# Weight rounding in a two-layer encoder trunk: from a ScalarE copy to a converting transfer from DRAM, from the eighth slab on

## The chip, the core and the metric

The kernel runs on one core of a Trainium2 chip. The metric is the device time of one execution in microseconds (us). Engines are named as in the profile: PE is TensorE (matmuls), DVE is VectorE, ACT is ScalarE, POOL is GpSimd, SP is SyncE, whose queue issues most transfers.

## What is computed

The reference is an encoder trunk of two layers over x, 512 tokens of 1024 features in float32. Layer 0 has a combined mixer (a state-space scan with 16 heads and an mLSTM with 8 heads, each forward and backward), layer 1 a gated linear attention. Each layer ends in a convolutional feed-forward block (FFN):

```
def _conv_ffn(h, w_up, conv_w, conv_b, w_down):
    u = _dwconv(h @ w_up, conv_w, conv_b)
    gate, val = jnp.split(u, 2, axis=-1)
    return (jax.nn.gelu(gate, approximate=True) * val) @ w_down

def reference(...):
    for i in range(DEPTH):
        h = _rmsnorm(x, norm_g[i, 0])
        h = _ssd_mlstm_mixer(h, ...) if i % 2 == 0 else _gla_mixer(h, ...)
        x = x + _rmsnorm(h, norm_g[i, 1])
        f = _conv_ffn(_rmsnorm(x, norm_g[i, 2]), ffn_w_up[i], ffn_conv_w[i], ffn_conv_b[i], ffn_w_down[i])
        x = x + _rmsnorm(f, norm_g[i, 3])
    return x
```

All of the work is float32, and almost all of it is products with weights.

## The kernel before

All weights are laid out in order of use as 234 slabs of 128 x 1024 float32 (512 KB). A slab holds eight 128 x 128 tiles, mostly one output row tile of a product. PE multiplies in the type fp32r (a rounded float32). To keep float32 accuracy each operand is split in two parts: `hi`, the value rounded to fp32r, and `lo`, what is left. `mm3` makes three matmuls of the parts: hi by hi, hi by lo, lo by hi.

`w_load(i)` asks for slab i on SP's queue into `raw` (W_RAW = 3 buffers). `w_prep` makes `hi` on ACT (`S.copy`) and `lo` on DVE (raw minus hi), each in W_SPLIT = 5 buffers. `w_take` keeps W_AHEAD = 4 slabs made ahead of the one in use. So slab i's `hi` and `lo` can be written when the last matmul of slab i-5 is done, and they are read when four more slabs have gone through PE.

Products run as `Job`s (one slab, one PSUM bank) or as `nat_job`s (two slabs, four blocks of tokens). When a job ends, DVE takes its PSUM bank out (`conv` does so first of all) and then works on the result in SBUF. The eight banks have three names: two `pj`, three `ps`, three `pm`. FFN jobs go round all eight in turn (`PA`), the projections of the layer 0 mixer use the two `pj` alone.

The mixer of layer 0 first projects (slabs 0 to 11), then makes rows of gates in a long chain of DVE operations (`gate_rows`), writes them to DRAM (`rowd`, `rowd2`, `decd`), and loads them back spread over the partitions (SP's `s<-rowd` transfers of 256 KB). POOL multiplies some of these (`s160`, `s186`, `s191`, `s163`), and adds sums of squares (`accx`) at the ends of stages. Slabs 12 to 14 are three of the convolved projections (`s96`, `s100`, `s104` are their banks taken out), and 15 to 18 the z projection. Slabs 0 to 68 belong to mixer 0, 69 to 134 to FFN 0, 135 to 167 to mixer 1, and 168 to 233 to FFN 1. Between stages the first four FFN jobs run on half the tokens together, so their four slabs are needed at once.

The program is written in Tile: a scheduler sets the order of each engine's instructions from the program and its own estimates, and puts in the semaphore waits. Each engine then runs its list strictly in that order. All calls go through a recording helper, so nearly every instruction carries its line, L105. Instructions are told apart by their tiles.

Of the kernel before, what the change touches and what calls it, by code (L numbers as in the profile page):

```python
# [16 lines left out]
P = 128  # L17
T = 512
# [11 lines left out]

# columns of the constant block
_C = {}
# [8 lines left out]
class _Balance:  # L41
    """Work issued so far to TensorE and VectorE, in ns, to weave two streams evenly."""

# [3 lines left out]
    def weave(self, streams, done):  # L47
        """streams: (generator, engine whose work it is paced by, total ns of that work, head start in ns).
        The stream least far along goes on, if what it needs is done."""
        st = [{"g": g, "e": e, "n": float(n), "t": -lead / float(n), "need": None} for g, e, n, lead in streams]  # L50
        while st:
            ok = [x for x in st if x["need"] is None or x["need"] in done]
            assert ok, [x["need"] for x in st]
            x = min(ok, key=lambda x: x["t"])
            t0 = getattr(self, x["e"])
            try:
                x["need"] = next(x["g"])
            except StopIteration:
                st.remove(x)
            x["t"] += (getattr(self, x["e"]) - t0) / x["n"]  # L60


class _Life:
    """First and last use of every work tile, in program order, and from that a slot for each."""

# [15 lines left out]
    def plan(self, slots):  # L81
        """The slot that has been free for longest."""
        until, res = [-1] * slots, []
        for a, z in zip(self.first, self.last):
            i = min(range(slots), key=lambda j: until[j])
            assert until[i] < a or until[i] < 0, "too few slots"
            until[i] = z + 1
            res.append(i)
        return res


class _Eng:
    """An engine that notes which tiles its instructions touch and how long they take."""

# [36 lines left out]
def kernel(ctx: ExitStack, tc: tile.TileContext, xin, wst, cst, dsk, gw2, out, life=None, plan=None):  # L131
# [47 lines left out]

# [1 line left out]
    cc = cp.tile([P, NCONST], F32, name="cc")  # L181
# [30 lines left out]

# [1 line left out]
    wstate = {"raw": {}, "next": 0, "ready": [], "unit": 0}  # L214
    NSLAB = wst.shape[0]

    def w_load(i):
        raw = wp.tile([P, 1024], F32, tag="raw", name=f"raw{i}", bufs=W_RAW)
        SY.dma_start(raw, wst[i])
        wstate["raw"][i] = raw  # L220

    def w_prep():
        i = wstate["next"]
        if i >= NSLAB:
            return
        wstate["next"] += 1
        if i not in wstate["raw"]:
            w_load(i)
        raw = wstate["raw"].pop(i)
        hi = wp.tile([P, 1024], F32R, tag="hi", name=f"hi{i}", bufs=W_SPLIT)  # L230
        lo = wp.tile([P, 1024], F32R, tag="lo", name=f"lo{i}", bufs=W_SPLIT)
        S.copy(hi, raw)
        V.tensor_tensor(lo, raw, hi, ALU.subtract)
        wstate["ready"].append((hi, lo))

    def w_take(n, width=P):
        """The next n tiles of `width` columns of the stream, as (hi, lo) pairs."""
        res = []
        for _ in range(n):
            c0 = wstate["unit"]  # L240
            i, o = divmod(c0, 1024)
            while len(wstate["ready"]) < i + 1 + W_AHEAD and wstate["next"] < NSLAB:
                w_prep()
            hi, lo = wstate["ready"][i]
            res.append((hi[:, o:o + width], lo[:, o:o + width]))
            wstate["unit"] += width
        return res

    def mm3(o, a, b, first, last):
        """o += a^T b with operands in two exact parts."""  # L250
        (ah, al), (bh, bl) = a, b
# [7 lines left out]
    class Job:  # L259
        """One 128-row tile of W^T h."""  # L260

# [37 lines left out]
    def run_group(jobs, r, mid=None, serial=False):  # L299
        """Several jobs together, one k tile after the other (or one job after the other)."""  # L300
        if not serial:
# [42 lines left out]
    def nat_job(h, post, hi=False):  # L344
        """256 columns of h^T W with tokens on the partitions."""
        w = w_take(KD, 256)
# [12 lines left out]

# [1 line left out]
    def col_sum(o, i, acc):  # L361
        """o[tok, 2i + t]: the sum of acc[:, tok] over the partitions, for two tiles of tokens."""
        for t in range(2):
            PE.matmul(o[:, 2 * i + t:2 * i + t + 1], acc[:, t * P:(t + 1) * P], ones[:, 0:1], start=True, stop=True)

    def rstd(v, rs):
        """rs = 1 / sqrt(v / D + eps) for columns v."""
        S.activation(rs, v, AF.Sqrt, bias=eps1, scale=1.0 / D)
        V.reciprocal(rs, rs)

    def spread(o, rs):
        """o[p, tok] = rs[tok] on every partition."""
        for t in range(2):
            PE.matmul(o[:, t * P:(t + 1) * P], rs[:, t:t + 1].broadcast_to((P, P)), ident, start=True, stop=True)

    def split(xk, g, h, n, r):
        """The two exact parts of x * g (the norm's per-token factor is applied to the products)."""
        if h[n] is None:
# [5 lines left out]
    class Scale:  # L384
        """1 / rms of x for every token: as columns [tok, tile] and as a row on all partitions."""

# [28 lines left out]
    class Post:  # L415
        """x += f * g * rstd, fed with f one row tile and one token half at a time."""

# [26 lines left out]
        def finish(self, r, nxt=None):  # L444
            """nxt: (layer, which, h) of the norm that follows."""
            o = ps()
# [10 lines left out]

# [1 line left out]
    def conv(o, sc, wc, b, taps):  # L459
        """Depthwise convolution along the tokens of a PSUM tile, scaled by token, into SBUF."""  # L460
        half = taps // 2
# [54 lines left out]

# [1 line left out]
    def mixer0(h, x_again, sc, chain_of):  # L518
        done = set()
        # small block: dt and gates  # L520
        smallj = {}
# [22 lines left out]

# [1 line left out]
        rows = {}  # L546
# [11 lines left out]
        def gate_rows():  # L558
# [6 lines left out]
            V.reciprocal(d, d)  # L565
            V.tensor_tensor(u, u, d, ALU.mult)           # z = e / (2 + e)
            z2 = st()
            S.activation(z2, u, AF.Square)
            V.tensor_scalar(d, z2, 2.0 / 15, 2.0 / 13, ALU.mult, ALU.add)
            for j in range(5, -1, -1):  # L570
                V.tensor_tensor(d, d, z2, ALU.mult)
                V.tensor_scalar(d, d, 2.0 / (2 * j + 1), None, ALU.add)
            V.tensor_tensor(u, u, d, ALU.mult)           # log1p(exp(-|g|))
            lo64, hi64 = slice(0, 64), slice(64, 128)
# [32 lines left out]
            yield  # L607
            # SSD rows
            cs = st()
# [13 lines left out]
            yield  # L623
            # mLSTM rows
            ig = st()
# [30 lines left out]
            S.activation(q4[hi64], fc[hi64], AF.Exp)  # L656
            # rows to DRAM for broadcasts over the partitions
            G.dma_start(rowd[lo64], cs[lo64])
# [7 lines left out]
            G.dma_start(dskb, dsk.broadcast_to((P, 16)))  # L666
            # columns: [tok, chunk, (quantity of the pair, direction), head]
            for w, tiles in ((16, (q1, q2)), (8, (q3, q4))):
# [10 lines left out]

# [1 line left out]
        zt = [[None] * 2 for _ in range(NCH)]  # L681
# [12 lines left out]

# [1 line left out]
        def b8(ap):  # L696
# [150 lines left out]

# [1 line left out]
        kT, qT = [None] * 8, [None] * 8  # L849
# [143 lines left out]

# [1 line left out]
        part = [None] * KD  # L995
# [45 lines left out]

# [1 line left out]
    def mixer1(h, x_again, sc, chain_of):  # L1043
# [34 lines left out]
        def after(ins, first):  # L1078
            """Issue order only: groups activations by their function table."""
            tc.add_manual_dep(ins.ins, first.ins.name, mybir.DependencyInfo(  # L1080
# [58 lines left out]
        def head(hd, ps):  # L1139
# [7 lines left out]
            for dd in range(2):  # L1147
                bcv = bcs[dd][hd]
                b3 = bcv.rearrange("p (c l) -> p c l", l=64)
                ei = 63 if dd == 0 else 0  # L1150
                # first / second 64 tokens of a block in the order of the scan
                fi, se = (0, 1) if dd == 0 else (1, 0)
# [10 lines left out]
                after(S.activation(ke, ke, AF.Exp, scale=1.0 / 16.0), pin["ln"])  # L1163
                # kc: keys of the first half to its end, of the second half as they are
                kc, q2 = st(), st()
# [18 lines left out]
                yield  # L1184
                # whole-block operands of the states
                d2 = dec.rearrange("p (c u) -> p c u", u=2)
# [84 lines left out]

# [1 line left out]
    def load_x(src):  # L1273
# [8 lines left out]
    def load_first(r):  # L1282
        """Half the tokens of x, two row tiles to a tile."""
        x = [st() for _ in range(KD // 2)]
# [69 lines left out]
W_SPLIT = 5  # L1354
W_AHEAD = 4
BANKS = {"pj": 2, "ps": 3, "pm": 3}
PA = ("pj", "pm", "ps", "ps", "pm", "pj", "pm", "ps")
# [6 lines left out]
def _layout(a):  # L1364
    """Host-side layout: transposed activations, weights in the order of use, packed vectors."""
    f = lambda n: np.asarray(a[n])
# [84 lines left out]
def build(new, arrays):  # L1451
    """The program: traced once to learn how long each tile is in use, then with a slot for each."""
    plan = None
# [25 lines left out]
```

## Time and profile before

| | |
|---|---|
| time, median of 3 runs | 1556.7 us (1555.45 to 1556.77) |
| span of the profiled execution | 1554.8 us |
| PE busy | 1508.2 us, 97% |
| DVE busy | 1032.1 us, 66% |
| ACT busy | 730.6 us, 47% |
| POOL busy | 142.8 us, 9% |
| bytes read from HBM | 146.42 MB |

The span goes from the first to the last instruction. The profile gives no other time for that execution, and the runs stand 0.7 to 2.0 us above its span. An engine's busy time is an average over stages: what an edit is worth has to be read in its stage.

### The profile page before, as it was taken

The numbers are of one execution on the slowest core, as the hardware profiler recorded it, in microseconds if no ns is written. First come the engines' busy times: TensorE is split into PE (matmuls) and PEld (weight loads), VectorE is DVE, ScalarE is ACT, GpSimd is POOL, SyncE is SP. The second block draws the span as 40 slices with busy tenths as digits, with TensorE's granted clock in tenths as the row PEclk, the third lists the DMA queues.
The fourth block names the chain that finished last, engine by engine and source line by source line (L and its number), as shares of the span: only waits on it lengthen the run. The fifth ranks groups of instructions, "written<-read, shape, count | busy, mean of one in ns | idle before, by whom it ended". The sixth has DMA issues, their size and how long they took to land.

```text
span 1554.8 us, 22022 instructions
## 1 busy us (share of the span) xinstructions
PE 1508.2 (97%) x8616; PEld 1300.3 (84%) x8616; DVE 1032.1 (66%) x1703; ACT 730.6 (47%) x1332; POOL 142.8 (9%) x165
## 2 busy tenths in 40 slices
PE   7989999999999999999999999999999999999997
PEld 6879887888987988888888997898899888888887
DVE  6986789967754888623676378737537974267744
ACT  6445545744642664423444356436545543244432
POOL 5020321212100110000000030000003000000000
PEclk9999999999999999999999999999999999999999
DMA  5243243334322322222222132211131322222211
GB/s 186 96 156 96 82 129 102 102 114 140 131 91 79 112 86 104 95 95 95 95 95 99 69 123 103 74 56 55 65 125 69 109 95 95 95 95 95 95 69 54
DMA packets 67303, 152.46 MB, mean 98 GB/s; under 512 B 6256, under 2 KB 32896, under 8 KB 67200
## 3 DMA queue, kind: packets, MB, share of 16 engines
q1 hardware_dynamic: 61984, 145.77, 27.7%
q10 hardware_dynamic: 4752, 4.23, 0.9%
q8 instruction: 67, 1.10, 0.3%
q0 software_dynamic: 464, 1.06, 0.2%
q14 instruction: 36, 0.29, 0.1%
HBM read 146.42 MB, written 4.59 MB: 97 GB/s over the span
## 4 chain that ended last, share of the span: by engine, by line
PE 80%; DVE 11%; ACT 4%; DMA 3%; issue 2%; POOL 0%; SPq 0%; DVEq 0%; ACTq 0%; POOLq 0%
PE pj L105 31%; PE ps L105 25%; PE pm L105 24%; DVE s L105 8%; DMA s<-rowd 2%; ACT s L105 2%; DVE lo L105 2%; DVE t L105 1%; ACT hi L105 1%; ACT L105 0%; DVE pacc L105 0%; DMA raw<-in_w 0%; POOL s L105 0%; ACT msq L105 0%; DVE rd L105 0%
## 5 line engine op out<-in xcount | busy, mean ns | idle before, releaser
L105 DVE TENSOR_TENSOR lo<-raw,hi 128x1024 fp32r<-128x1024 f32 x234 | 291.4, 1249 | 220.5 <-ACT hi L105 220.3
L105 PE MATMUL pj<-s,hi 128*128 128x512 f32 (+1 forms) x1384 | 405.4, 376 | 5.2 <-ACT s L105 5.2
L105 ACT CAST hi<-raw 128x1024 fp32r<-128x1024 f32 x234 | 244.3, 1048 | 241.7 <-PE pj L105 107.7
L105 PE MATMUL pm<-s,hi 128*128 128x512 f32 (+1 forms) x1140 | 309.9, 357 | 8.4 <-ACT s L105 6.8
L105 PE MATMUL ps<-s,hi 128*128 128x512 f32 (+1 forms) x1140 | 307.3, 356 | 0.7 <-DVE t L105 0.7
L105 PEld LDWEIGHTS pj<-s,hi 128*128 128x128 f32 x1384 | 248.7, 189 | 54.6 <-ACT s L105 5.6
L105 PE MATMUL pj<-s,lo 128*128 128x512 f32 (+1 forms) x692 | 257.3, 372 | 0.0
L105 PE MATMUL pj<-hi,s 128*128 128x256 f32 x1280 | 241.6, 286 | 6.6 <-DVE s L105 3.0
L105 PEld LDWEIGHTS pm<-s,hi 128*128 128x128 f32 x1140 | 202.7, 190 | 41.6 <-ACT s L105 6.8
L105 PEld LDWEIGHTS ps<-s,hi 128*128 128x128 f32 x1140 | 202.2, 190 | 33.2 <-issue 1.1
L105 PEld LDWEIGHTS pj<-hi,s 128*128 128x128 f32 x1280 | 200.4, 189 | 9.1 <-DVE s L105 3.6
L105 PE MATMUL ps<-s,lo 128*128 128x512 f32 (+1 forms) x570 | 203.0, 356 | 1.2 <-DVE lo L105 1.2
L105 PE MATMUL pm<-s,lo 128*128 128x512 f32 (+1 forms) x570 | 203.1, 356 | 0.0
L105 PE MATMUL pj<-lo,s 128*128 128x256 f32 x640 | 180.7, 282 | 0.0
L105 DVE SCALAR_TENSOR_TENSOR s<-s,cc,s 128x511 f32<-128x511 f32 (+1 forms) x240 | 168.0, 712 | 3.2 <-ACT s L105 0.8
L105 ACT ACTIVATE s<-s 128x512 f32<-128x512 f32 (+1 forms) x145 | 90.3, 629 | 154.8 <-DVE s L105 137.0
L105 DVE TENSOR_TENSOR s<-s,s 128x512 f32<-128x512 f32 (+3 forms) x214 | 136.3, 651 | 34.0 <-ACT s L105 31.9
L105 PEld LDWEIGHTS pj<-s,lo 128*128 128x128 f32 x692 | 130.6, 189 | 23.8 <-issue 1.0
L105 ACT ACTIVATE s<-s,cc 128x512 f32<-128x512 f32 (+2 forms) x188 | 121.8, 664 | 38.2 <-DVE s L105 37.3
L105 PEld LDWEIGHTS ps<-s,lo 128*128 128x128 f32 x570 | 108.2, 190 | 17.6 <-DVE lo L105 1.6
L105 PEld LDWEIGHTS pj<-lo,s 128*128 128x128 f32 x640 | 121.5, 190 | 1.5 <-issue 1.0
L105 PEld LDWEIGHTS pm<-s,lo 128*128 128x128 f32 x570 | 108.3, 190 | 15.8
(155 smaller groups left out, 1342.5 us busy)
## 6 DMA issues: line engine op xcount, KB each, us to landing
raw<-in_w SPq DMA_DIRECT2D x234, 512.0 KB, 3.2
s<-rowd SPq DMA_DIRECT2D x64, 256.0 KB, 3.8
s<-in_x SPq DMA_DIRECT2D x8, 256.0 KB, 6.0
s<-in_x ACTq DMA_DIRECT2D x16, 128.0 KB, 2.7
xsave<-s SPq DMA_DIRECT2D x16, 128.0 KB, 2.3
s<-xsave ACTq DMA_DIRECT2D x16, 128.0 KB, 2.4
out_x<-s SPq DMA_DIRECT2D x16, 128.0 KB, 1.8
rowd<-s POOLq DMA_DIRECT2D x3, 128.0 KB, 2.3
```

The costliest lines, as they stand in the source:

```text
L105: return f(*a, **k)
```

## The change

From slab 8 on (`W_ACT = 8`) `hi` is no longer written by ACT. `w_load` issues a second transfer of the same slab from DRAM, on POOL's queue, whose target has the type fp32r, so the transfer rounds. `lo` is made on DVE as before, now from two transferred tiles. Slabs 0 to 7 stay with ACT. The other lines of the diff remove comments.

```
     def w_load(i):
         raw = wp.tile([P, 1024], F32, tag="raw", name=f"raw{i}", bufs=W_RAW)
         SY.dma_start(raw, wst[i])
-        wstate["raw"][i] = raw
+        hi = None
+        if i >= W_ACT:
+            hi = wp.tile([P, 1024], F32R, tag="hi", name=f"hi{i}", bufs=W_SPLIT)
+            G.dma_start(hi, wst[i])
+        wstate["raw"][i] = raw, hi
 ...
-        raw = wstate["raw"].pop(i)
-        hi = wp.tile([P, 1024], F32R, tag="hi", name=f"hi{i}", bufs=W_SPLIT)
+        raw, hi = wstate["raw"].pop(i)
+        if hi is None:
+            hi = wp.tile([P, 1024], F32R, tag="hi", name=f"hi{i}", bufs=W_SPLIT)
+            S.copy(hi, raw)
         lo = wp.tile([P, 1024], F32R, tag="lo", name=f"lo{i}", bufs=W_SPLIT)
-        S.copy(hi, raw)
         V.tensor_tensor(lo, raw, hi, ALU.subtract)
 ...
+W_ACT = 8
```

226 casts leave ACT, 226 issues come to POOL, and the scheduler sets DVE's, PE's and SP's instructions anew around them. Three places show it.

POOL's list after the gate rows, before the change (`s150` is the spread copy of `decd`, and the four products multiply rows loaded from `rowd2`):

```order
L105 DMA decd_1407<-dec129_1256 128x4
L105 DMA rowd2_513<-s87_920 64x512
L105 DMA s150_1409<-decd_1407 128x512
L105 TENSOR_TENSOR s160_1450<-s160_1450,s67_614 128x512
L105 TENSOR_TENSOR s186_1548<-s186_1548,s69_647 128x512
L105 TENSOR_TENSOR s191_1594<-s191_1594,s69_647 128x512
L105 TENSOR_TENSOR s163_1463<-s163_1463,s67_614 128x512
```

The same place of POOL's list with the change:

```order
L105 DMA rowd2_513<-s87_920 64x512
L105 DMA hi15_783<-in_w 128x1024
L105 DMA hi16_939<-in_w 128x1024
L105 DMA s150_1409<-decd_1407 128x512
L105 TENSOR_TENSOR s160_1450<-s160_1450,s67_614 128x512
L105 TENSOR_TENSOR s186_1548<-s186_1548,s69_647 128x512
L105 TENSOR_TENSOR s191_1594<-s191_1594,s69_647 128x512
L105 DMA hi17_981<-in_w 128x1024
L105 DMA hi18_1023<-in_w 128x1024
L105 TENSOR_TENSOR s163_1463<-s163_1463,s67_614 128x512
```

The transfers of slabs 15 and 16 now stand behind the issue of `rowd2`, and those of 17 and 18 behind three products that each wait for a loaded row.

DVE's list at the same time of the program, before the change (`pj95`, `pj99` and `pj103` are the banks of slabs 12, 13 and 14):

```order
L105 TENSOR_TENSOR lo16_940<-raw16_937,hi16_939 128x1024
L105 TENSOR_TENSOR s96_968<-pj95_943,srow9_127 128x512
L105 TENSOR_TENSOR lo17_982<-raw17_979,hi17_981 128x1024
L105 SCALAR_TENSOR_TENSOR s97_970<-s96_968,cwh43_238,s97_970 128x510
L105 SCALAR_TENSOR_TENSOR s97_970<-s96_968,cwh43_238,s97_970 128x511 x2
L105 SCALAR_TENSOR_TENSOR s97_970<-s96_968,cwh43_238,s97_970 128x510
L105 TENSOR_TENSOR s100_1010<-pj99_985,srow9_127 128x512
```

DVE's list there with the change:

```order
L105 TENSOR_TENSOR lo16_941<-raw16_937,hi16_939 128x1024
L105 TENSOR_TENSOR s96_968<-pj95_943,srow9_127 128x512
L105 SCALAR_TENSOR_TENSOR s97_970<-s96_968,cwh43_238,s97_970 128x510
L105 SCALAR_TENSOR_TENSOR s97_970<-s96_968,cwh43_238,s97_970 128x511 x2
L105 TENSOR_TENSOR lo17_983<-raw17_979,hi17_981 128x1024
L105 SCALAR_TENSOR_TENSOR s97_970<-s96_968,cwh43_238,s97_970 128x510
L105 TENSOR_TENSOR s100_1010<-pj99_985,srow9_127 128x512
```

`lo17` has moved behind three operations of the convolution, and it still stands ahead of `s100`, which takes the next bank out.

DVE's list in FFN 0, before the change (two jobs: one bank taken out into `s930`, the next into `s933`):

```order
L105 TENSOR_TENSOR s930_7169<-ps929_7144,srow42_237 128x512
L105 TENSOR_TENSOR lo111_7179<-raw111_7176,hi111_7178 128x1024
L105 SCALAR_TENSOR_TENSOR s931_7171<-s930_7169,cc_72,s931_7171 128x511 x2
L105 TENSOR_TENSOR s933_7207<-pj932_7182,srow42_237 128x512
L105 TENSOR_TENSOR lo112_7221<-raw112_7218,hi112_7220 128x1024
L105 SCALAR_TENSOR_TENSOR s934_7209<-s933_7207,cc_72,s934_7209 128x511 x2
```

The same two jobs with the change:

```order
L105 TENSOR_TENSOR s930_7169<-ps929_7144,srow42_237 128x512
L105 SCALAR_TENSOR_TENSOR s931_7171<-s930_7169,cc_72,s931_7171 128x511 x2
L105 TENSOR_TENSOR lo111_7180<-raw111_7176,hi111_7178 128x1024
L105 TENSOR_TENSOR s933_7207<-pj932_7182,srow42_237 128x512
L105 SCALAR_TENSOR_TENSOR s934_7209<-s933_7207,cc_72,s934_7209 128x511 x2
```

In each FFN job `lo` has gone from directly behind the taking out of the bank to behind the convolution's two operations.

## Rows read from the trace of the kernel before

**Rows 1.** The page: busy us of each engine, share of the span, instructions.

```profile
PE 1508.2 (97%) x8616; PEld 1300.3 (84%) x8616; DVE 1032.1 (66%) x1703; ACT 730.6 (47%) x1332; POOL 142.8 (9%) x165
```

**Rows 2.** Windows: busy us of PE, PEld, DVE, ACT, POOL; clock, DMA share, GB/s.

```profile
76.00:112.00 36.00, 31.36 (x181) 27.42 (x179) 31.00 (x42) 15.55 (x27) 8.66 (x9) 0.95 0.49 157
112.00:545.00 433.00, 419.54 (x2697) 368.91 (x2697) 318.81 (x622) 228.97 (x537) 77.02 (x65) 1.00 0.34 107
545.00:895.00 350.00, 349.58 (x1651) 289.26 (x1650) 212.63 (x279) 146.32 (x199) 6.59 (x10) 1.00 0.26 93
895.00:1200.00 305.00, 298.01 (x2059) 270.66 (x2059) 194.79 (x378) 157.90 (x318) 30.40 (x38) 0.99 0.24 82
```

**Rows 3.** DVE's timeline in FFN 0: start, us, operation, idle before it.

```profile
752.62 0.69 DVE L105 TENSOR_TENSOR s<-pj,srow 128x512 f32<-128x512 f32 x1 [2.02 <-PE pj L105]
753.47 1.23 DVE L105 TENSOR_TENSOR lo<-raw,hi 128x1024 fp32r<-128x1024 f32 x1 [0.16 <-ACT hi L105]
```

**Rows 4.** The page's groups: count, busy, mean ns, idle before by releaser.

```profile
L105 DVE TENSOR_TENSOR lo<-raw,hi 128x1024 fp32r<-128x1024 f32 x234 | 291.4, 1249 | 220.5 <-ACT hi L105 220.3
...
L105 ACT CAST hi<-raw 128x1024 fp32r<-128x1024 f32 x234 | 244.3, 1048 | 241.7 <-PE pj L105 107.7
```

**Rows 5.** The chain that ended last, by line, whole span.

```profile
PE pj L105 31%; PE ps L105 25%; PE pm L105 24%; DVE s L105 8%; DMA s<-rowd 2%; ACT s L105 2%; DVE lo L105 2%; DVE t L105 1%; ACT hi L105 1%; ACT L105 0%; DVE pacc L105 0%; DMA raw<-in_w 0%; POOL s L105 0%; ACT msq L105 0%; DVE rd L105 0%
```

**Rows 6.** That chain in order of time: start, us, what.

```profile
62.83 1.06 ACT hi L105
63.92 1.23 DVE lo L105
...
92.29 0.93 ACT hi L105
...
415.26 0.94 ACT hi L105
...
741.47 5.56 PE ps L105 x24
```

**Rows 7.** DMA issues (KB each, median us to landing), and POOL's time for one.

```profile
raw<-in_w SPq DMA_DIRECT2D x234, 512.0 KB, 3.2
s<-rowd SPq DMA_DIRECT2D x64, 256.0 KB, 3.8
...
s<-decd POOLq DMA_DIRECT2D x1, 256.0 KB, 5.7
...
s<-in_g POOLq DMA_DIRECT2D x1, 128.0 KB, 2.4
...
L105 POOL DMA_DIRECT2D rowd<-s x3 | 1.7, 562 | 44.9 <-DVE s L105 33.0 <-DVE ue L105 11.2 <-ACT s L105 0.7
```

**Rows 8.** POOL's timeline after the gate rows.

```profile
90.22 0.54 POOL L105 DMA_DIRECT2D rowd<-s  x1 [0.73 <-ACT s L105]
...
99.54 1.29 POOL L105 TENSOR_TENSOR s<-s,s 128x512 f32<-128x512 f32 x1 [7.79 <-DMA s<-rowd]
103.10 3.01 POOL L105 TENSOR_TENSOR s<-s,s 128x512 f32<-128x512 f32 x2 [2.27 <-DMA s<-rowd]
```

**Rows 9.** DVE's timeline there: slabs 16 and 18, banks of slabs 12 and 14.

```profile
93.26 1.22 DVE L105 TENSOR_TENSOR lo<-raw,hi 128x1024 fp32r<-128x1024 f32 x1 [0.63 <-ACT hi L105]
96.75 0.69 DVE L105 TENSOR_TENSOR s<-pj,srow 128x512 f32<-128x512 f32 x1 [2.27 <-PE pj L105]
...
98.78 4.17 DVE L105 SCALAR_TENSOR_TENSOR s<-s,cwh,s 128x510 f32<-128x510 f32 x4
...
104.87 2.32 DVE L105 TENSOR_TENSOR lo<-raw,hi 128x1024 fp32r<-128x1024 f32 x1
...
111.04 0.68 DVE L105 TENSOR_TENSOR s<-pj,srow 128x512 f32<-128x512 f32 x1
```

**Rows 10.** Start of FFN 0: `lo` of slab 72 on DVE, and PE's idle time.

```profile
528.25 1.22 DVE L105 TENSOR_TENSOR lo<-raw,hi 128x1024 fp32r<-128x1024 f32 x1
...
534.46 0.48 PE L105 MATMUL ps<-s,hi 128*128 128x256 f32 x2 [0.33 <-DVE t L105]
```

## The prediction

> **What bounds the kernel now.** I read the page's busy times first. PE is busy for 1508.2 of 1554.8 us [rows 1], so only 46.6 us of the span can be won by any edit that leaves the matmuls alone, and ACT, from which this change takes work, is at 47%. The windows by stage say where those 46.6 us lie. FFN 0 (545 to 895) has 0.4 us of idle PE in 350. The gate stage (76 to 112) has 4.6, the rest of mixer 0 (112 to 545) 13.5 and mixer 1 with its ends 7.0 [rows 2]. That makes 25.1 us of idle PE between 76 and 1200; what is left lies mostly at the start, which the change doesn't touch, and at the end. Then I read the chain of waits. The casts `ACT hi` have 1% of it and the loads `s<-rowd` 2% [rows 5]. The cast is 1.05 us long and there are 234 of them, 244.3 us of ACT in all [rows 4]. Nearly all of that lies beside other work: DVE waits 220.3 us for casts, which looks large, but DVE has room, and in FFN 0 it waits before a `lo` for only 0.16 us after having waited 2.02 us for PE [rows 3].
>
> **What a slab's new `hi` costs.** POOL issues the transfer when slab i-5 has left PE. One issue keeps POOL for 0.56 us. No row has a converting transfer, so I bound its time to landing. SP's transfer of the same 512 KB takes 3.2 us, and POOL's of 128 KB takes 2.4. The longer end is POOL's 256 KB at 5.7, which ran beside other loads [rows 7]. So from free buffer to landed `hi` it is 3.8 to 6.3 us where the cast took 1.05. I take 5, between the ends, because in the mixers other loads run beside it.
>
> **The FFN stages: nothing.** A job is 24 matmuls in 5.56 us [rows 6]. Four slabs are made ahead, so `hi` and `lo` have 4 x 5.56 = 22.2 us from the free buffer to their first use, and need 5 + 1.25 (the `lo` of [rows 4]). DVE's list lets the convolution go first and then waits for `hi`; the next bank is taken out 1 or 2 us late, and FFN jobs come back to a bank only after eight jobs, 44 us. DVE is busy for 212.6 of 350 us [rows 2], so the delay doesn't pile up. The cover fails when `hi` takes over 20 us, and then each slab costs what is over. The second transfer doubles the weight traffic of this stage to some 0.52 of DMA time (0.26 in [rows 2]), which still fits.
>
> **ACT relieved: -3.5 us.** Behind six casts of the chain there stands other ACT or PE work and no `lo`; the first is the 0.93 us at 92.29 and the last the 0.94 us at 415.26, six in all, 5.7 us [rows 6]. Bounds: 0, if the next chain is as long, and 5.7. I take 3.5, since the chains in the mixers run close together. Casts that have a `lo` behind them (62.83 is one) save nothing: a transfer takes their place.
>
> **The gate chain: +1 us.** `lo12` starts 1.1 us after its cast began at 62.83 [rows 6]. With the change its `hi` lands at 66.6 to 69.1, and the list puts four short operations (2.3 us) ahead of it, so DVE comes to it at about 66.2. That is a wait of 0.4 to 2.9 us, in a chain of DVE operations on which PE waits later. Part of it goes into work that only changes places. I take 1; bounds 0 and 2.5.
>
> **POOL's list at slabs 15 to 18: +4.5 us.** This is the term that I trust most in direction. `hi15` and `hi16` stand behind the issue of `rowd2` at 90.22 [rows 8], so they go out at about 90.8 and 91.4 and the second lands at 95 to 97. `lo16`, which ran at 93.26, ends at about 98.2, and the bank of slab 12, taken out at 96.75, is 1.4 us late [rows 9]. Then three of the four convolution operations (4.17 us for four) bring DVE to `lo17` at 101 to 102. But `hi17` stands on POOL behind three products that wait for loads from `rowd2`, the last of which ended at 103.10 + 3.01 = 106.1 [rows 8]. SP's list now asks for those loads ahead of slab 18, so I let them end at about 102, with 99 and 104 as ends. `hi17` lands 5 us after that, at 107 (104 to 109), and DVE stands for 2 to 8 us. Behind it on DVE are the taking out of the banks of slabs 13 and 14, the only two banks that the projections have. The z projection needs them, and before the change PE went on when the second was free at 111.04 [rows 9]. So PE is late by nearly what DVE is late; `lo18`, which took 2.32 us beside POOL's products, gives back 1. Bounds: 1 and 7.6. From there PE is almost never idle until the middle of mixer 0, so it cannot catch up.
>
> **The stage starts: +1 us.** At the start of an FFN four slabs are needed at once. `lo72` ran at 528.25, and PE was idle for 0.33 us soon after [rows 10]. DVE's list now has it behind some ten operations of the norm. I count 0.33 for each of three such starts; bounds 0 and 2.5 each. `accx` stands behind `hi73` on POOL, which waits for the last job of the mixer; that job is done when `accx` begins, so I count nothing (1 us each if it is late).
>
> **The loads `s<-rowd`: +2 us.** They have 2% of the chain, 31 us [rows 5], at a median of 3.8 us each [rows 7]. A second stream of weights takes another 0.26 of DMA time. If every such overlap doubled the load's time it would be 31 x 0.26 = 8 us; if the engines have room, 0. I take a quarter. The Trainium skill (DMA: Bandwidth & Descriptors, "Issuing engines are not separate DMA queues") says that transfers of all issuing engines run on the same 16 engines and interleave. By that rule POOL's queue gives `hi` no path of its own and the term would lie nearer 8, for a sum 6 us higher; no row of this trace separates the two.
>
> **Sum.** -3.5 + 1 + 4.5 + 1 + 2 = +5.0 us on a span of 1554.8, which is 1559.8. The median of the runs stands 1.9 us above that span, so **1562 us** in round numbers.
>
> **Rivals.** *Faster, 1549.* The loads from `rowd2` come early enough, and `hi17` is there when DVE wants it. The point that decides is the end of the third product: before about 96 (102 less the 5 to 6 us that `hi` takes) the stall is gone. Then all six casts count (5.7 us) and with them four casts ahead of a `lo` at 1.05 each, 9.9 in all, less the 2 us of the loads: 1556.7 - 7.9. For it speaks that SP's list moved these loads up; against it that the first product ended at 100.8 [rows 8].
> *No change, 1556.7.* What ACT gives back equals what the waits take, each 3 to 4 us, because PE's idle 25.1 us are shared by many chains. FFN's even rows speak for it, the gate stage against it.
> *Late transfers, 1578.* DVE and POOL get in each other's way: `lo18` took 2.32 us where the mean is 1.25, while POOL's two products ran from 103.10 on [rows 4, 8, 9]. If DVE's work holds up POOL's writing of a transfer as well, or if converting is slow, `hi` takes some 4 us more. Then slabs 15 to 18 cost 4 more, the gate chain 2, three stage starts 2 each, and the 94 slabs of the mixers some 4 in all: 1562 + 16. Beside it stands a rule of the Trainium skill (SBUF — State Buffer, "Who interferes with whom"): vector operations in a two-port mode lock GpSimd out of a shared port, so transfers issued from GpSimd wait for their descriptors. By that rule it comes out so; the lengthened `lo18` shows the two engines meeting, and no row shows it for descriptors.
>
> **Chances.** The forecast's case has 0.45, with a range of its own from 1557 to 1569. Faster has 0.25, no change 0.17, late transfers 0.13. About 0.2% (3.1 us) is what a measurement of this kernel can tell from no change. Slower holds 0.40 of the forecast's case and the late transfers' 0.13, which is 0.53. Faster is 0.24 and same 0.23 (no change less a little, the forecast's low end, and the weak end of the faster case). The range from 1549 to 1578 leaves out the outer half of the faster case and of the late transfers, 0.19.
>
> **What the profile would show.** If I am right, the page has 8 casts on ACT and some 490 us of ACT busy. In FFN 0 PE stays at 349 to 350 of 350 us and DVE's idle time before `lo` moves from casts to the transfer `hi<-in_w`. Near 102 to 108 DVE stands before `lo17` for several us, with POOL's product just ahead of the issue, and PE's z projection starts at about 116, not 112. `hi<-in_w` lands 4 to 6 us after its issue. I am wrong if that start is at 112 or earlier, if FFN jobs leave 5.56 us, or if a converting transfer takes 3 us or over 10.

## The result, and the profile after

The changed kernel takes 1607.5 us (median of 4 runs, 1604.4 to 1617.2) against 1556.1 for the kernel before on the same chip: a ratio of 1.0344, 95% interval 1.0313 to 1.0375. It is 51.5 us slower. The prediction said slower, but 1562, with a range that ended at 1578.

Lines of the page after, which answer to [rows 1, 4, 7]: busy times, bytes, the group of `lo`, and three kinds of transfer (KB each, median us from issue to landing).

```profile
PE 1522.8 (95%) x8616; PEld 1309.8 (82%) x8616; DVE 1029.4 (64%) x1703; ACT 514.2 (32%) x1106; POOL 263.5 (16%) x391
...
HBM read 264.91 MB, written 4.59 MB: 168 GB/s over the span
...
L105 DVE TENSOR_TENSOR lo<-raw,hi 128x1024 fp32r<-128x1024 f32 x234 | 289.1, 1237 | 270.9 <-DMA hi<-in_w 205.8
...
raw<-in_w SPq DMA_DIRECT2D x234, 512.0 KB, 4.0
hi<-in_w POOLq DMA_DIRECT2D x226, 512.0 KB, 4.4
s<-rowd SPq DMA_DIRECT2D x64, 256.0 KB, 4.5
```

ACT has lost 226 casts (514.2 us busy, forecast some 490), and `hi` lands 4.4 us after its issue, inside the forecast 4 to 6. PE makes the same 8616 matmuls and is busy for 14.6 us more; its idle time in the span has grown from 46.6 to 81.2 us. The span is 49.2 us longer (1604.0 against 1554.8): 34.6 of idle PE and 14.6 of slower matmuls.

The windows of the changed kernel below are cut where PE has made about as many matmuls as at the ends of those of [rows 2], so they are the same stages: gate stage, the rest of mixer 0, FFN 0, mixer 1 with its ends, FFN 1.

```profile
74.00:117.00 43.00, 34.16 (x179) 29.38 (x177) 31.14 (x43) 9.29 (x20) 10.96 (x14) 0.88 0.60 188
117.00:582.00 465.00, 429.27 (x2700) 376.82 (x2701) 320.46 (x627) 180.36 (x485) 107.16 (x119) 0.97 0.53 162
582.00:932.00 350.00, 348.89 (x1647) 288.46 (x1646) 209.63 (x273) 83.39 (x131) 39.41 (x72) 1.00 0.56 185
932.00:1248.00 316.00, 301.70 (x2063) 272.03 (x2062) 194.12 (x381) 123.87 (x284) 52.09 (x79) 0.98 0.45 143
1248.00:1604.00 356.00, 344.35 (x1622) 284.81 (x1620) 212.81 (x295) 81.56 (x127) 30.10 (x57) 0.99 0.53 178
```

Against [rows 2] the gate stage is 7 us longer, the rest of mixer 0 is 32, FFN 0 is 0, and mixer 1 with its ends is 11. In mixer 0 PE needs 429.3 us for some 2700 matmuls where it needed 419.5, and stands for 35.7 us where it stood for 13.5. The granted clock there is 0.97 of its upper level, 2.4 GHz, where it was 1.00; in FFN 0, without idle time, it is 1.00 in both. So the clock's share of the loss follows the idle time: it appears where PE has stood.

One link of the chain of waits in mixer 0 shows how the time goes (start, us, what).

```profile
231.05 1.23 POOL s L105
232.28 6.01 DMA hi<-in_w
238.28 0.02 issue
238.31 1.23 DVE lo L105
239.53 1.77 DVE s L105 x2
...
242.68 7.49 DMA s<-rowd
...
250.26 3.49 ACT s L105 x10
253.74 0.16 ACT mst_c L105
253.90 0.04 issue
253.94 1.23 PE pm L105 x4
```

A product on POOL lets the next `hi` go out, DVE stands until it has landed and has made `lo`, the work queued behind `lo` comes late, a load from `rowd` after that, and at the end PE waits. The like stands in the chain at 375.34, where a `hi` has 6.29 us.

At that point I had three theories. **Queue**: POOL's list couples transfers and products, each of which waits behind the other. **Late**: a `hi` is there some 3.4 us later than a cast (the medians 4.4 less 1.05, counted from the start of the issue and of the cast), and DVE stands in front of `lo` with other work behind. **Traffic**: the second stream of weights slows the other transfers. The experiments weigh them. Each is read against the kernel before as it was timed beside it (1556.1 to 1557.4).

### The profile page after: what moved, and what is told of

It is laid out like the page before. It is cut to its first block, busy times and chain, and to the rows that moved or that the text cites. A ratio compares the mean times of both kernels' runs of the same rounds, so it can differ in the third digit from the quotient of the medians.

```text
span 1604.0 us, 22147 instructions
## 1 busy us (share of the span) xinstructions
PE 1522.8 (95%) x8616; PEld 1309.8 (82%) x8616; DVE 1029.4 (64%) x1703; ACT 514.2 (32%) x1106; POOL 263.5 (16%) x391
## 4 chain that ended last, share of the span: by engine, by line
issue 40%; PE 27%; DVE 12%; DMA 12%; POOL 5%; ACT 2%; POOLq 0%; SPq 0%; DVEq 0%; ACTq 0%
PE pj L105 16%; DMA hi<-in_w 8%; DVE s L105 8%; PE pm L105 6%; PE ps L105 6%; POOL hi L105 4%; DMA s<-rowd 3%; DVE lo L105 3%; ACT s L105 2%; POOL s L105 1%; DVE t L105 1%; DMA raw<-in_w 1%; DVE pacc L105 0%; DMA rowd<-s 0%; POOL accx L105 0%
## 5 line engine op out<-in xcount | busy, mean ns | idle before, releaser
L105 POOL DMA_DIRECT2D hi<-in_w x226 | 120.9, 535 | 1004.6 <-PE pj L105 488.4
L105 PE MATMUL pj<-hi,s 128*128 128x256 f32 x1280 | 247.4, 290 | 12.2 <-DVE s L105 7.5
L105 PEld LDWEIGHTS pj<-hi,s 128*128 128x128 f32 x1280 | 204.5, 193 | 16.0 <-DVE s L105 8.6
```

The lines of the kernel that those rows point to most:

```text
L105: return f(*a, **k)
```

## The experiments

**Which slabs cost.** Four kernels use the transfer for some slabs alone. In place of `i >= W_ACT` the condition is `by_dma(i)`, which has one of these lines in each:

```diff
+def by_dma(i):                               # mixer0_only
+    return 8 <= i < 69
+    return 135 <= i < 168                    # mixer1_only
+    return 69 <= i < 135 or i >= 168         # ffn_only
+    return 73 <= i < 131 or 172 <= i < 230   # ffn_inner
```

> The hi transfer only for slabs 8 to 68 (mixer 0). In the changed kernel lo 68 to 72 start 36 to 37 us later than before, so 'queue', 'late' and 'traffic' all say 1592 (1586 to 1597). If the parts don't add up (this, mixer 1 alone and the FFNs alone), the stages help each other to the loss.

Measured: 1597.0 against 1556.6, ratio 1.0251 (1.0211 to 1.0291), +40.4. All three theories said so, and it separates none of them.

> The hi transfer only for slabs 135 to 167 (mixer 1). In the changed kernel the lo starts fall back from 40 us behind at slab 134 to 49 at slab 166, so about 1565 (1558 to 1569). Mixer 1 has few products on POOL and no loads from rowd: 'queue' and 'traffic' say the low end, 1557 to 1560; 'late' says 1563 to 1567.

Measured: 1563.5, ratio 1.0044 (1.0030 to 1.0058), +6.9. That lies in what "late" gave, and above what the others gave.

> The hi transfer only for the FFN slabs (69 to 134 and 168 to 233), the cast on ScalarE for all mixer slabs. Theory 'queue' (POOL's list holds transfers and the mixers' products, each waiting behind the other) and theory 'late' (a hi lands 4 to 6 us after its free buffer where the cast took 1.05, and DVE stands before lo where a mixer has no slack) both put the loss into the mixers and the two FFN starts: 1556 plus about 3 at each FFN start, 1556 to 1564. Theory 'traffic' (the second weight stream slows the other transfers, the loads from rowd above all) gives the same here, since the FFNs have slack. Over 1570 would say that the FFN slabs carry a loss that the lo starts of the changed kernel don't show.

Measured: 1569.3, ratio 1.0073 (1.0049 to 1.0098), +12.7, above what was expected.

> The hi transfer only for the inner slabs of the FFNs (73 to 130 and 172 to 229), the cast for the first four and last four of each. The matmuls of ffn_only fell back at the ends and starts of stages (2 us at the start of FFN 0, 2 and 4 around the start of mixer 1, 3.5 at the start of FFN 1) and by nothing inside. If the loss is where slabs are wanted at once and a transfer's 4 us stand in the chain, this is 1554 to 1559. If the transfers of the inner slabs cost too, 1562 or more.

Measured: 1559.4 against 1556.8, ratio 1.0014 (1.0002 to 1.0026), +2.6. So some 10 of the FFNs' 12.7 us belong to their first and last four slabs, and little, if anything, to the other 116. The three parts add up to 60.0 us, where the whole change costs 51.5: they overlap a little, and mixer 0 is by far the largest.

What happens at such an edge is in the chain of waits of ffn_only, at the end of FFN 0:

```profile
885.56 2.39 PE pj L105 x20
887.95 0.28 issue
888.24 3.56 DMA hi<-in_w
891.79 0.04 issue
891.84 0.51 PE pj L105 x2
```

The last jobs there run on half the tokens, and PE comes to a `hi` that has not landed. In POOL's timeline of the changed kernel, at the start of FFN 0, the last four transfers go out one by one as the last jobs of the mixer release their buffers:

```profile
554.47 0.53 POOL L105 DMA_DIRECT2D hi<-in_w  x1 [14.93 <-PE pm L105]
558.19 0.53 POOL L105 DMA_DIRECT2D hi<-in_w  x1 [3.19 <-DVE s L105]
561.03 0.53 POOL L105 DMA_DIRECT2D hi<-in_w  x1 [2.31 <-DVE s L105]
563.86 0.53 POOL L105 DMA_DIRECT2D hi<-in_w  x1 [2.31 <-PE pm L105]
567.89 6.72 POOL L105 TENSOR_TENSOR accx<-accx,t 128x256 f32<-128x256 f32 x7 [3.50 <-ACT t L105]
```

**The traffic alone.** The kernel before, casts kept, and every slab from 8 on is asked for a second time on SP's queue, right behind `raw`. The second copy isn't used.

```diff
-        SY.dma_start(raw, wst[i])
+        first = SY.dma_start(raw, wst[i])
+        if i >= 8:
+            spare = wp.tile([P, 1024], F32, tag="spare", name=f"spare{i}", bufs=1)
+            second = SY.dma_start(spare, wst[i])
+            tc.add_manual_dep(second.ins, first.ins.name, ...)   # order only
-NS_BUFS = 64
+NS_BUFS = 62
```

> The kernel before with its casts, and from slab 8 on a second transfer of every slab on SP's queue right behind raw, into a spare tile that nobody reads (62 work slots in place of 64 to make room). This adds the traffic of the change without its waits. 'queue' and 'late': 1556 to 1562 (SP's issue of 0.4 us stands ahead of some loads). 'traffic': 1585 or more, with the loads s<-rowd at 4.5 us or more where they took 3.8.

Measured: 1572.2, ratio 1.0099 (1.0076 to 1.0122), +15.7, between the two. The transfers of its page, and what SP waited for:

```profile
raw<-in_w SPq DMA_DIRECT2D x234, 512.0 KB, 3.7
spare<-in_w SPq DMA_DIRECT2D x226, 512.0 KB, 4.5
s<-rowd SPq DMA_DIRECT2D x64, 256.0 KB, 4.7
```

```profile
SPq L105 <- DMA spare<-in_w: 178.4, 77, 5.6
```

`s<-rowd` takes as long as in the changed kernel, at a third of the loss. But SP stands for 178.4 us in the whole span for the one spare tile (the 23 us that the next expectation names are those from 112 to 440 us). So a second form sends the second copy from DRAM to DRAM, with four buffers: `dp.tile(..., bufs=4)` in place of `wp.tile(..., bufs=1)`, and 64 slots.

> As traffic_only, but the second transfer of each slab goes from DRAM to DRAM scratch with four buffers, and the work slots stay at 64: in traffic_only SP itself waited 23 us for the one spare tile, which the change has no part in. If the 14 us of traffic_only came from the traffic, they stay (1568 to 1575); if from SP standing before the spare tile, 1556 to 1562.

Measured: 1569.6, ratio 1.0070 (1.0047 to 1.0094), +12.2, in runs from 1560.5 to 1572.3. The profile is of the 1560.5 run, whose `s<-rowd` took 5.7 us, so the length of these loads by itself doesn't set the time. Traffic is worth something, at most a dozen us or so in these forms, which also issue 226 transfers more on SP. It isn't most of the 51.5.

**POOL's products.** `VG` is VectorE under a name that the kernel's own count of DVE's work, by which it paces its streams, leaves out. The 64 products and sums of the mixers go there, in the kernel before (the control) and in the changed one.

```diff
+    VG = _Eng(nc.vector, life)
-                G.tensor_tensor(qs, qs, qT[hd], ALU.mult)
+                VG.tensor_tensor(qs, qs, qT[hd], ALU.mult)
 ...   (so at six more places)
```

> The control for the next run: the kernel before, with the 64 products and sums of the mixers that POOL computes moved to VectorE (POOL keeps its sums of squares and its transfers). DVE has room on average, but gains some 60 us of work in the mixers: 1556 to 1575.

Measured: 1552.5 against 1557.4, ratio 0.9971 (0.9959 to 0.9984): 5.0 us faster than the kernel before, and below what was expected.

> The changed kernel with the same 64 operations moved to VectorE, so that in the mixers POOL's list holds hardly anything but transfers, and no product waits behind one or holds one up. The time and transfer of each hi stay. Read against the control: 'queue' says at most 20 us more than the control (what is left is the FFN starts and a part of the waits before lo); 'late' says 40 to 55 more, as between the changed kernel and before.

Measured: 1590.3, ratio 1.0211 (1.0193 to 1.0228), 37.8 us above its control. The transfers cost 13.7 less than with the products on POOL. "Queue" had said at most 20 above the control, "late" 40 to 55; most of the loss stays.

**A buffer more.** The sixth `hi` buffer lets slab i's transfer go out when slab i-6 is done. The same edit stands at the cast of slabs 0 to 7.

```diff
-            hi = wp.tile([P, 1024], F32R, tag="hi", name=f"hi{i}", bufs=W_SPLIT)
+            hi = wp.tile([P, 1024], F32R, tag="hi", name=f"hi{i}", bufs=W_SPLIT + 1)
-NS_BUFS = 64
+NS_BUFS = 62
```

> The changed kernel with six hi buffers in place of five (62 work slots in place of 64), so that hi of slab i may be asked for when slab i-6 has left PE, one slab sooner. 'late' says that most of the waits before lo go: 1556 to 1580. 'queue' says that the products still stand behind transfers, though for less long: 1580 to 1600. If neither counts, it stays at 1604 or more.

Measured: 1579.6 against 1557.4, ratio 1.0150 (1.0124 to 1.0176). The loss falls from 51.5 to 22.2. The time itself falls by 27.9, to the border between what "late" and "queue" gave. The loads from `rowd` stay as long as they were, so it isn't their length that the buffer gives back:

```profile
s<-rowd SPq DMA_DIRECT2D x64, 256.0 KB, 4.6
```

Two controls: the sixth buffer for `lo` instead, and the sixth `hi` buffer in the kernel before.

> The changed kernel with six lo buffers and five hi (62 work slots, as six_hi). If six_hi gained because hi is asked for one slab sooner ('late'), this gains nothing: 1600 to 1612. If it gained from the other slots or a freer order on DVE, this gains as well: 1575 to 1590.

Measured: 1615.4, ratio 1.0389 (1.0357 to 1.0422). A sixth `lo` buffer gains nothing. This kernel has the same 62 slots and as many buffers as `six_hi`, and against it `six_hi` is 35.8 us faster.

> The kernel before (casts on ScalarE) with six hi buffers and 62 work slots. 'late': a cast of 1.05 us has hardly a lateness to lose, so 1553 to 1559. If the sixth buffer itself is worth much whatever writes hi, 1530 to 1545.

Measured: 1564.8 against 1556.8, ratio 1.0053 (1.0035 to 1.0071): under casts the kernel with the sixth `hi` buffer is 8.0 us slower, not the same. No run shows why. Read against 1564.8, the transfer costs 14.8 with six buffers where it costs 51.5 with five, 36.7 less. So what one buffer hides of the lateness is 27.9 us by the time itself and 35.8 or 36.7 by the two controls. The waits of DVE in mixer 0 (56 to 560 us: total, times, longest) go with it, for the kernel before, the changed one, `six_hi` and `six_hi_before`:

```profile
DVE lo L105 <- ACT hi L105: 43.5, 28, 4.3
```

```profile
DVE lo L105 <- DMA hi<-in_w: 51.3, 24, 6.5
```

```profile
DVE lo L105 <- PE pj L105: 29.6, 9, 6.6
...
DVE lo L105 <- DMA hi<-in_w: 9.2, 7, 3.8
```

```profile
DVE lo L105 <- ACT hi L105: 0.7, 1, 0.7
```

Before the change DVE already stood 28 times in front of `lo` for a cast, and with a sixth buffer under casts it hardly does, so what stood behind these waits was the release of a `hi` buffer, with the cast of 1.05 us after it. Taking them away made that kernel no faster. In `six_hi` the tile `hi` is mostly there, and what ends most of the wait is PE's release of the buffer of `lo`.

These waits by themselves are far from the whole loss. From before to after they grow by 7.8 us only. DVE's idle time in the rest of mixer 0 grows from 114.2 to 144.5 us (the windows above and in [rows 2]), and most of that growth stands in front of other work: in the same view DVE's waits for `s` of ACT go from 12.8 to 25.1 us, those for the loads from `rowd` from 12.4 to 20.0. The lateness is passed on, and these views don't say by which way.

One rival was not run by itself: the order of DVE's list, which the scheduler makes anew for each kernel. The change put 157 of the 234 `lo` later in that list, and `six_hi` puts 164 earlier again, as well as asking for `hi` sooner. Against the order as the main cause speak, weakly, `six_lo`, where 35 `lo` stand earlier and nothing is gained, and `lo_later` below, where 43 stand later and nothing is lost. PE stood for a `lo` for only 0.8 us in mixer 0 of the changed kernel. No run has the new order with the old time of `hi`.

> Six hi buffers and the 64 operations of POOL on VectorE together. If 'late' (28 us by six_hi) and 'queue' (13 us by the pair of products_dve) are separate parts of the loss: 1579.6 less 13 and less the 5 that the control gains, 1560 to 1566. If they are one and the same waits: 1575 to 1580. What then is left above the control's 1552 is traffic and the FFN starts.

Measured: 1565.3, ratio 1.0075 (1.0047 to 1.0102). The number is the one expected of separate parts, but the control was the wrong one. With the last run it reads otherwise.

> The control products_dve_before (casts on ScalarE, the 64 operations on VectorE, 1552.4) with six hi buffers and 62 work slots. If the buffer gives a cast nothing, 1550 to 1555, the same as without it; under 1548 it would be a better version still.

Measured: 1549.2 against 1556.8, ratio 0.9952 (0.9936 to 0.9968). This is the fastest version of the study, 7.6 us under the kernel before, with the casts on ACT. Its page shows POOL at 61.0 us of work in place of 142.8 and PE busy for nearly all of the span:

```profile
PE 1507.7 (98%) x8616; PEld 1300.8 (84%) x8616; DVE 1035.5 (67%) x1767; ACT 732.8 (47%) x1332; POOL 61.0 (4%) x101
```

It gives the fourth corner. What the transfer costs (median with it less median with casts, the same buffers and the same place of the products; the scheduler's order differs):

| | products on POOL | products on VectorE |
|---|---|---|
| five `hi` buffers | 1607.5 - 1556.1 = 51.5 | 1590.3 - 1552.5 = 37.8 |
| six `hi` buffers | 1579.6 - 1564.8 = 14.8 | 1565.3 - 1549.2 = 16.1 |

With six buffers the transfer costs the same wherever the products are, as far as these medians can tell (each difference is good to some 3 to 5 us). So "queue" doesn't look like a part of its own: the products seem to pass on the lateness of `hi`. The times themselves warn against reading more into it. In the changed kernel the sixth buffer takes off 27.9 us with the products on POOL and 24.9 without, and moving the products takes off 17.2 with five buffers and still 14.3 with six. Under casts that move takes off 3.6 with five and 15.6 with six. With six buffers the products on POOL thus cost some 15 us whatever writes `hi`, for a reason that no run shows.

**Two that moved nothing.** In `lo_later` the program writes `lo` of a slab one slab later than the requests for `raw` and `hi`. In `raw_four` W_RAW is 4 and NS_BUFS 62.

```diff
+            while len(wstate["ready"]) < min(i + W_AHEAD, NSLAB):   # lo_later: was i + 1 + W_AHEAD
+                w_lo()
 ...
-W_RAW = 3                                                          # raw_four
+W_RAW = 4
```

> The changed kernel with raw and hi asked for as before, but lo of a slab written in the program one slab later (made three slabs ahead of use, not four), so that DVE's list has other work between the request and lo. Transfers, traffic and buffers are the same. 'late' in the form 'DVE stands before lo with other work queued behind it': 1565 to 1590. If it is PE that lacks lo, or the products on POOL ('queue'), or 'traffic': 1600 or more.

Measured: 1605.7, ratio 1.0319 (1.0294 to 1.0344). This says little: in the traces only 46 of the 234 `lo` changed their place in DVE's list, since the scheduler sets it by its own estimate of when `hi` is there.

> The changed kernel with four raw buffers in place of three (62 work slots). On SP's queue the next raw stands behind lo of the slab whose buffer it takes (168.8 us of SP's waits from 112 to 440 us, 124.3 before), and the loads from rowd stand behind raw. If this link passes the lateness of hi on to POOL's products and DVE, a buffer more breaks it: 1580 to 1597. If not, 1602 or more.

Measured: 1610.2, ratio 1.0349 (1.0326 to 1.0371). That the lateness is passed on through SP's queue, by `raw` ahead of the loads from `rowd`, was my reading of the chain at 242.68; this run speaks against it as the way that counts.

**The largest term by itself.** The condition is `15 <= i <= 18`.

> The hi transfer for slabs 15 to 18 alone (gate stage and z projection), the cast everywhere else. This measures by itself the term that the prediction put at 4.5 us (1 to 7.6). The lo starts of the changed kernel fall back from 1.6 us at slab 12 to 8.7 at slab 18 and 11.1 at 21. 'queue', which is what the prediction had here: 1558 to 1566. 'late': with only four transfers almost all of the mixer's waits are gone, so no more than that either. 1556 to 1558 would say that the delay is taken up again later in the mixer when the casts are back.

Measured: 1565.3 against 1557.0, ratio 1.0052 (1.0037 to 1.0067), +8.3 (5.8 to 10.4).

## Why the prediction was wrong, step by step

The direction was right and the size a tenth: 5.3 us above the kernel before were forecast, 51.5 were measured. The step that failed is the one on ACT, below, where a late `hi` in the mixers was put at nothing. (The 25.1 us of idle PE between 76 and 1200 leave out the 0.4 of FFN 0; they are 25.5, and nothing hangs on it.)

**FFN stages, 0: right.** 350 us for FFN 0 before and after, and 2.6 us for all 116 inner slabs of both FFNs.

**`hi` lands 3.8 to 6.3 us after its buffer is free: right in the median.** From the start of the issue it is 4.4, and 3.4 to 7.8 over all 226. The changed kernel's transfers in FFN 0 (600 to 900 us):

```profile
raw<-in_w SPq DMA_DIRECT2D x55, 512.0 KB, 4.4
hi<-in_w POOLq DMA_DIRECT2D x54, 512.0 KB, 4.3
```

POOL's converting transfer takes no longer than SP's plain one of the same slab, with DVE busy for 60% of the stage (209.6 of 350 us). The rival *late transfers* (1578) stood on transfers of some 9 us, and they aren't that slow. The rule beside it (the Trainium skill, SBUF — State Buffer, "Who interferes with whom") would have transfers of GpSimd wait while vector operations in a two-port mode hold a shared port; no row here shows that.

**POOL's list at slabs 15 to 18, +4.5: right in its mechanism, short in size.** POOL's, DVE's and PE's timelines there:

```profile
90.19 1.13 POOL L105 DMA_DIRECT2D hi<-in_w  x2
...
99.91 4.24 POOL L105 TENSOR_TENSOR s<-s,s 128x512 f32<-128x512 f32 x3 [8.05 <-DMA s<-rowd]
104.10 1.12 POOL L105 DMA_DIRECT2D hi<-in_w  x2
```

```profile
97.31 2.52 DVE L105 TENSOR_TENSOR lo<-raw,hi 128x1024 fp32r<-128x1024 f32 x2 [6.50 <-DMA hi<-in_w]
...
107.94 1.23 DVE L105 TENSOR_TENSOR lo<-raw,hi 128x1024 fp32r<-128x1024 f32 x1 [2.45 <-DMA hi<-in_w]
109.09 0.75 DVE L105 SCALAR_TENSOR_TENSOR s<-s,cwh,s 128x510 f32<-128x510 f32 x1
109.75 0.69 DVE L105 TENSOR_TENSOR s<-pj,srow 128x512 f32<-128x512 f32 x1
```

```profile
110.49 0.39 PE L105 MATMUL pj<-hi,s 128*128 128x256 f32 x1 [2.22 <-DVE s L105]
...
117.17 0.39 PE L105 MATMUL pj<-hi,s 128*128 128x256 f32 x1 [2.05 <-DVE s L105]
```

`hi17` stands behind the three products, goes out at 104.10 and lands at 107.92 (forecast: 107, within 104 to 109). DVE stands for 2.45 us (2 to 8), and PE's second step of the z projection starts at 117.2 (116). What was short is the first part: `hi15` and `hi16` went out from 90.19 on, about as forecast, but landed 7.0 and 7.8 us after their issues, above the 6.3 that I took as the longest. DVE stood 6.50 us in front of `lo15`, and the two `lo` ended at 99.8 (98.2). Alone the term measured 8.3 (5.8 to 10.4); its bounds were 1 and 7.6, where 2 to 8 less the 1 given back would have been 1 to 7.

**The gate chain, +1: about right.** DVE stood 0.73 us before `lo12` (0.4 to 2.9), which started 1.6 us later than before; what that cost was not measured alone. The whole gate stage lost 7 us, with the term above in it.

**The stage starts, +1: wrong, too small.** PE's windows with equal numbers of matmuls around the start of FFN 0, of mixer 1 and of FFN 1 (length, PE busy, clock, DMA share, GB/s), before:

```profile
500.00:560.00 60.00, 58.04 (x451) 1.00 0.29 98
895.00:960.00 65.00, 63.31 (x402) 0.97 0.36 122
1165.00:1220.00 55.00, 53.12 (x340) 0.97 0.24 84
```

And after the change:

```profile
532.80:596.40 63.60, 59.48 (x451) 0.97 0.51 167
932.30:1001.20 68.90, 63.93 (x402) 0.98 0.57 189
1209.60:1268.10 58.50, 53.63 (x340) 0.97 0.52 170
```

They cost 3.6, 3.9 and 3.5 us, 11.0 in all, over the upper bound of 7.5. `ffn_only` less `ffn_inner`, 10 us, says the like. I took 0.33 us from an idle time of PE [rows 10]. What fits in size is the transfer itself, though no run tests it alone: four slabs are wanted at once, little lies between the last release and their use, and `hi` comes 4.3 - 1.05 = 3.3 us later than a cast.

**The loads `s<-rowd`, +2: probably too small, size open.** They went from 3.8 to 4.5 us. The second stream alone cost 12.2 and 15.7 in two forms that load SP more than the change does. The rule cited there (DMA: Bandwidth & Descriptors, "Issuing engines are not separate DMA queues" of the Trainium skill) agrees in direction: `raw` on SP's queue went from 3.2 to 4.0 while POOL's queue carried `hi`. What is left of the change with six buffers, 14.8 to 16.1 us, is of that size, but the stage edges are in it as well.

**ACT relieved, -3.5: the step that failed.** It said that a cast with a `lo` behind it saves nothing, since "a transfer takes their place", and I put no price on that exchange outside the slabs named. Only a rival put a price on the 94 slabs of the mixers, "some 4 in all", for a `hi` four us later still. The measured price is what the sixth buffer hides, 28 to 37 us. `mixer0_only` shows the same from the other side: the slabs of mixer 0 cost 40.4, of which slabs 15 to 18 alone cost 8.3, and for most of the other 32 the sum had no term. The trace of before had the row for a bound, had I read the waits by stage: DVE stood 28 times in mixer 0 in front of `lo` for a cast. A `hi` that takes 3.4 us longer gives up to 28 x 3.4 = 95 us there. I had read the 220 us of such waits for the whole span [rows 4] and let FFN 0 speak for all of it. The bound is a loose one: by the traces DVE's waits for `hi` in mixer 0 grew by only 7.8 us, and the rest of the loss came out elsewhere. Whether the forecast relief of ACT was there at all no run separates.

**The rivals.** *Faster* needed the third product to end before about 96; it ended at 104.15, and the first began only at 99.91. *No change* fell with it: the loss is nine times the 5.7 us that ACT could give at most.

**The clock.** 14.6 us of the loss are the same matmuls at a lower granted clock, in the stages where PE stood more. No term held that. A loss of idle time in PE costs more than itself here, by 14.6 / 34.6, some two fifths.

What stays open: how the last 15 us divide between traffic and stage edges, by which of the chains between DVE, POOL, SP and ACT most of the lateness reaches PE, and how much of it belongs to the new order of the lists.

## What to carry to other kernels

When an on-chip copy is replaced by a transfer, count per stage how often its reader already stands waiting for that copy behind a buffer just released; each of those places can take up to the difference in latency (3.4 us here), however idle the engines look, and the delay need not show in front of that reader. A buffer more, so that the request goes out a step earlier, hid 28 to 37 of 51 us; moving other work off the issuing queue brought the loss to 37.8, and with the buffer as well to 16.1. Price the edges of stages by the transfer's own time; here each cost 3.5 to 3.9 us.

## What the runs showed of the hardware that I had not expected

In FFN 0 a converting transfer of 512 KB by POOL's queue landed in 4.3 us where a plain one by SP's took 4.4. Over the whole span it took 4.4, and the plain second transfer of `traffic_only` 4.5. So the conversion cost nothing that can be seen. PE's 8616 matmuls took 1522.8 us at a mean granted clock of 0.984 where they took 1508.2 at 0.992 before; the product of the two is the same within 0.2%.
